# A hybrid decoder step on one core: three edits to what GpSimd issues and to where one stage's value tiles lie

## Chip, cores and metric

The kernel runs on one core of a Trainium2 chip. The metric is the device time of one launch in microseconds (us). Three runs are timed and their median counts; one further execution is profiled, and all rows below are from it.

## The reference, cut to what matters

One layer of a decoder step, in float32, for 512 prompt tokens and for 8 samples of 4 new tokens each; all share the weights.

```
x += 0.5 * SwiGLU_1(RMSNorm(x))
h  = RMSNorm(x); [q|k|v|u] = h @ W_in
x += concat(RMSNorm(DilatedAttn(q,k,v)), RMSNorm(S5_GLU(u))) @ W_out
x += 0.5 * SwiGLU_2(RMSNorm(x))
x += sigmoid(RMSNorm(x) @ W_gate) * (p @ W_ple)
```

Three places matter here. The prompt's attention (8 heads, 512 x 512, in three dilated branches) adds a bias that depends on distance. The samples' attention multiplies softmax weights with gathered rows of a value cache of 2048 positions. The state-space branch ends in a gated unit `z * sigmoid(z @ w_glu + b)`, whose output is normalised by its mean square over 512 channels.

## The kernel before

All 544 tokens stand in the free dimension, channels on the 128 partitions. Every large product goes through `mm_tile` (line 194): a weight tile is split into a high and a low part (`whi` on ScalarE, line 175; `wlo` on VectorE, line 176) and three products are summed. The program has three parts: the first SwiGLU, a mixed part, and the output projection with the second SwiGLU and the rest.

The change is in the mixed part. There each engine runs its instructions in the order in which the code is written, and that order is given by the hand-written table `ORDER`, which calls steps of several generators in turn: `M`/`E` (a matmul tile and what empties it), `SQ` and `B` (the samples' scores), `SA`/`SB` (state space), `aq`/`at`/`ap` (the prompt's attention: scores and softmax, transposes, products with the values), `O0`/`O1` (`sample_out` for samples 0 to 3 and 4 to 7, called the first and the second group here) and others. An instruction that waits holds back everything behind it on its engine. TensorE is PE in the profile, VectorE DVE, ScalarE ACT, GpSimd POOL; PEld is TensorE's weight load.

What the edits touch:

- `load_bt(hp)` (line 1003) fetches the two bias tiles `bt` (256 KB each) of head pair `hp` from DRAM scratch into buffers of the pool `sp5`, 8 buffers that `L`, `pt`, `kb1` and `kt1` share. It is called once before the first unit of `att_q` and then behind the last of the four units of each head pair. Line 1020 reads the tiles; lines 1022 and 1025 are the two passes of the softmax on ScalarE.
- `sample_out(gr)` runs nine steps n = 0 to 8 per group. Each multiplies two value tiles `vv` (e = 0, 1; 512 KB each, line 1178) with weights in `pz` (line 1191). `load(n + 1)` stands ahead of the products of step n. The tiles lie in `wkp`, 6 buffers of which `pz` holds one.
- `sample_scores` streams 32 key tiles `kk` (512 KB, line 1073) through the 4 buffers of `kkp` and query rows `qb` (line 1088) through 2; line 1099 multiplies and line 1100 reduces. All this is done before the second group's first step.
- `glu(m)` (four tiles) squares its output on ScalarE (line 251 for the first, 254 for the others) and adds squares in `Stat.add` (line 255). Line 1220 makes the gated output, line 299 (ScalarE) and line 300 (VectorE) split it.

GpSimd has no other work in the mixed part than to issue the loads of `kk`, `kb1`, `qb`, `bt` and `vv`, in the order of the table, and to add the squares of the gated unit. Weights and results go through SyncE's queue.

Of the kernel before, what the change touches and what calls it, by code (L numbers as in the profile page):

```python
# [18 lines left out]
P = 128  # L19
# [9 lines left out]
DA = 512  # L29
# [73 lines left out]
def decoder_step(ctx: ExitStack, tc: tile.TileContext, a: dict, o: list):  # L103
    nc = tc.nc
    V, A, PE, SP, Q = nc.vector, nc.scalar, nc.tensor, nc.sync, nc.gpsimd

    def dram(t, off, dims):
        return bass.AP(tensor=t.tensor, offset=t.offset + off, ap=dims)
# [6 lines left out]
    def sb(pool, shape, name, dt=F32, **kw):  # L115
        return pool.tile(shape, dt, name=name, **kw)

    qD = dpool.tile([NS, DA], F32, name="qD")
    btD = dpool.tile([NH, P, 641], F32, name="btD")
# [192 lines left out]
    def s2(shape, name, dt=F32):  # L312
        return cur["s2"].tile(shape, dt, name=name, tag="s2")

    def psm(shape=None, name="sm"):
        return cur["sm"].tile(shape or [P, 512], F32, name=name, tag="sm")
# [425 lines left out]
    with ExitStack() as st:  # L742
# [7 lines left out]
        wk = lambda shape, name: wkp.tile(shape, F32, name=name, tag="wk")  # L750
        s5 = lambda shape, name: sp5.tile(shape, F32, name=name, tag="s5")
        kk2 = lambda name: kkp.tile([P, 2, DA], F32, name=name, tag="kk")
# [245 lines left out]
        bts, Ls, pts = {}, {}, {}  # L998

        def load_bt(hp):  # L1000
            for e in range(2):
                bts[hp, e] = s5([P, 512], "bt")
                Q.dma_start(bts[hp, e], dram(btD, (2 * hp + e) * P * 641 + 127, [[640, P], [1, 512]]))

        def att_q():
            load_bt(0)
            yield
            for u, (hp, i) in enumerate(units):
                w = (i + 1) * P
                pss, mns = [], []  # L1010
                for e in range(2):
                    pr = slice(64 * e, 64 * e + 64)
                    ps = psm()
                    PE.matmul(ps[:, :w], qT[pr, hp, i * P:(i + 1) * P], kT[pr, hp, 0:w], start=True, stop=True)
                    pss.append(ps)
                for e in range(2):
                    Ls[u, e] = L = s5([P, 512], "L")
                    mn = sb(small, [P, 4], "mn", bufs=4)
                    mns.append(mn)
                    V.tensor_tensor_reduce(L[:, :w], pss[e][:, :w], bts[hp, e][:, 512 - w:], -1.0, 3e38, ALU.add,  # L1020
                                           ALU.min, mn[:, 0:1])
                    A.activation(L[:, :w], L[:, :w], AF.Exp, scale=-1.0, bias=mn[:, 0:1], accum_out=mn[:, 1:2])  # L1022
                for e in range(2):
                    V.reciprocal(mns[e][:, 2:3], mns[e][:, 1:2])
                    A.activation(Ls[u, e][:, :w], Ls[u, e][:, :w], AF.Copy, scale=mns[e][:, 2:3])
                if i == 3 and hp < 3:
                    load_bt(hp + 1)
                yield
# [104 lines left out]
        def sample_out(gr):  # L1133
            sc = scs[gr]
            s3 = lambda i, n=P: sc[:n, i].rearrange("p b (t h) -> p (b t) h", h=NH)
            bq = lambda t: t[:, None, :].to_broadcast([P, 16, NH])
            fs = lambda i, n=P: sc[:n, i].rearrange("p b x -> p (b x)")
            V.tensor_tensor(s3(0), s3(0), bq(bfar), ALU.add)
            V.tensor_tensor(s3(1), s3(1), bq(bnear), ALU.add)
            mx = s2([P, P], "mx")  # L1140
            V.tensor_tensor(mx, fs(1), fs(2), ALU.max)
            V.tensor_tensor(mx, mx, fs(0), ALU.max)
            V.tensor_tensor(mx[:NS], mx[:NS], fs(3, NS), ALU.max)
            yield
            ps = psm()
            PE.transpose(ps[:, :P], mx, ident)
            m1 = sb(small, [P, 4], "m1", bufs=2)
            V.tensor_reduce(m1[:, 0:1], ps[:, :P], AX.X, ALU.max)
            dg = sb(small, [P, P], "diag", bufs=2)
            V.tensor_scalar(dg, ident, m1[:, 0:1], None, ALU.mult)  # L1150
            yield
            pm = psm()
            PE.matmul(pm[:, :P], ones, dg, start=True, stop=True)
            for i, n_ in ((0, P), (1, P), (2, P), (3, NS)):
                V.tensor_tensor(fs(i, n_), fs(i, n_), pm[:n_, :P], ALU.subtract)
            pz = wk([P, 2, 4, 160], "pz")
            pz = [pz[:, i] for i in range(2)]
            dv = lambda t: t.rearrange("p b (t x) -> p b t x", x=40)[:, :, :, 0:8]
            s4v = lambda i, n=P: sc[:n, i].rearrange("p b (t h) -> p b t h", h=NH)
            for i in range(2):  # L1160
                V.memset(pz[i], 0.0)
                A.activation(dv(pz[i]), s4v(i), AF.Exp)
            A.activation(fs(2), fs(2), AF.Exp)
            A.activation(fs(3, NS), fs(3, NS), AF.Exp)
            yield
            su = s2([P, 4, 4, 8], "su")
            V.tensor_tensor(su, s4v(2), dv(pz[1]), ALU.add)
            V.tensor_tensor(su, su, dv(pz[0]), ALU.add)
            V.tensor_tensor(su[:NS], su[:NS], s4v(3, NS), ALU.add)
            order = [None] + [(j, f) for j in range(DS) for f in range(2)]  # L1170
            vld = {}

            def load(n):
                if n < len(order):
                    r0, step = (1920, 1) if n == 0 else ((order[n][0], 16), (1536 + order[n][0], 4))[order[n][1]]
                    vld[n] = [wk([P, 2, DA], "vv") for _ in range(2)]
                    for e in range(2):
                        Q.dma_start(vld[n][e], dram(cv, ((4 * gr + 2 * e) * PAST + r0) * DA,  # L1178
                                                    [[step * DA, P], [PAST * DA, 2], [1, DA]]))
            load(0)  # L1180
            yield
            ps = psm()
            PE.matmul(ps[:, 0:1], su.rearrange("p b t h -> p (b t h)"), ones[:, 0:1], start=True, stop=True)
            V.reciprocal(m1[:, 1:2], ps[:, 0:1])
            po = psm([P, 512], "po")
            for n, jf in enumerate(order):
                load(n + 1)
                v_ = vld.pop(n)
                for b in range(4):
                    lt = sc[:, 2, b] if n == 0 else pz[jf[1]][:, b, 32 * jf[0]:32 * jf[0] + 32]  # L1190
                    PE.matmul(po[32 * b:32 * b + 32, :], lt, v_[b // 2][:, b % 2, :], start=n == 0, stop=n == len(order) - 1)  # L1191
                if n == 0:
                    for b in range(4):
                        PE.matmul(po[32 * b:32 * b + 32, :], sc[:NS, 3, b], vs, start=False, stop=False)
                yield
            rv = s2([P, NH, HD], "rvv")
            V.scalar_tensor_tensor(rv, po.rearrange("p (h d) -> p h d", d=HD), m1[:, 1:2],
                                   sel_h[:, :, None].to_broadcast([P, NH, HD]), ALU.mult, ALU.mult)
            yield
            pf = psm([P, 4, 16], "pf")  # L1200
            for m in range(4):
                PE.matmul(pf[:, m, :], rv[:, 2 * m:2 * m + 2, :].rearrange("p h d -> p (h d)"), sel_t, start=True, stop=True)
            V.tensor_copy(att[:, :, S + 16 * gr:S + 16 * gr + 16], pf)
            yield

        ssm_st, att_st = Stat(DA, (Q,)), Stat(DA)
        att_st.accs.append(sb(small, [P, NT], "sacc", bufs=2))
        att_sq = att_st.accs[0][:, :S]
        rs = {1: ssm_st, 0: att_st}
# [247 lines left out]
def run_tile(nc, args, outs):  # L1457
    with tile.TileContext(nc, schedule_with_timeline_sim=TS) as tc:
        with tc.manual_schedule(engines=ENG):
            decoder_step(tc, args, outs)  # L1460
# [18 lines left out]
```

## Time and profile before

| | |
|---|---|
| timed runs, us | 1302.9, 1295.39, 1298.36 (median 1298.36) |
| profiled execution, us | 1290.02 |
| its span, us | 1288.2 |
| busy share of the span: TensorE, VectorE, ScalarE, GpSimd | 94%, 55%, 35%, 9% |
| mixed part in the span, about | 440 to 770 us |

The span is the time from the first to the last record of the profile; 1.8 us of the profiled execution lie around it. The busy share is an average: TensorE is at its peak in both SwiGLU parts and below it in the mixed part.

### The profile page before, as it was taken

The page shows a single profiled execution, that of the slowest core. Times are in us where ns is not written, and L with a number is a line of the kernel's source. Part 1 is how long each engine was busy: PE and PEld are TensorE (multiplying, and loading weights), DVE is VectorE, ACT ScalarE, POOL GpSimd, SP SyncE. Part 2 cuts the span into 40 slices and gives each one's busy share as a digit, 9 for nine tenths or more (in the row PEclk, how much of TensorE's full clock was granted, in tenths as well). Part 3 has the DMA queues.
Part 4 walks back from the last instruction along what each step waited for, and adds up shares of the span by engine and source line. Part 5 has one row for each costly group of instructions (what it writes and reads, how often), then busy time and mean ns, then how long its engine had stood idle before and what let it go on. Part 6 is the DMA issues. An engine that isn't in the chain of part 4 may idle for free.

```text
span 1288.2 us, 23223 instructions
## 1 busy us (share of the span) xinstructions
PE 1208.3 (94%) x9518; PEld 1142.4 (89%) x9518; DVE 713.5 (55%) x1499; ACT 446.1 (35%) x889; POOL 121.8 (9%) x195
## 2 busy tenths in 40 slices
PE   8999999999999999994769889999999999999995
PEld 7899999999999988983645449999999999999994
DVE  5544478476447638777775548444433444444455
ACT  5333322322233323121754445333322223333344
POOL 2200000233000112110123311000000000000000
PEclk8999999999999998996979989999999999999998
DMA  8484566668546549766358855445566455222321
GB/s 248 134 260 147 173 217 226 227 198 258 191 167 207 170 138 299 233 203 218 91 207 243 255 172 191 155 144 199 174 217 231 153 192 180 80 83 77 93 64 70
DMA packets 207547, 231.30 MB, mean 180 GB/s; under 512 B 8647, under 2 KB 187735, under 8 KB 206416
## 3 DMA queue, kind: packets, MB, share of 16 engines
q1 hardware_dynamic: 189552, 170.35, 40.8%
q0 software_dynamic: 17856, 59.45, 14.3%
q8 instruction: 75, 1.23, 0.4%
q14 instruction: 32, 0.26, 0.1%
q10 hardware_dynamic: 32, 0.01, 0.0%
HBM read 217.46 MB, written 81.89 MB: 232 GB/s over the span
## 4 chain that ended last, share of the span: by engine, by line
PE 81%; DMA 6%; DVE 5%; issue 4%; ACT 3%; POOL 1%; SPq 0%; ACTq 0%; POOLq 0%; DVEq 0%
PE acc L194 72%; DMA vv<-in_cache_v_dram 2%; DMA raw<-in_w_in_dram 1%; PE acc L206 1%; PE acc L1441 1%; DVE kk L1099 1%; DMA raw<-in_ffn_w_up_dram 1%; DMA pc<-pD 1%; PE sm L915 1%; PE po L1191 1%; DMA mm<-mD 1%; PE sm L910 1%; PE sm L263 1%; POOL vv L1178 1%; ACT L L1022 1%
## 5 line engine op out<-in xcount | busy, mean ns | idle before, releaser
L194 PE MATMUL acc<-xh,whi 128*128 128x272 f32 x1888 | 398.5, 292 | 5.9 <-DVE qT L773 1.3
L194 PE MATMUL acc<-xl,whi 128*128 128x272 f32 x1888 | 393.9, 290 | 0.7 <-DVE xl L304 0.3
L194 PE MATMUL acc<-xh,wlo 128*128 128x272 f32 x1888 | 393.4, 289 | 0.9 <-DVE wlo L176 0.9
L175 ACT CAST whi<-raw 128x512 fp32r<-128x512 f32 (+2 forms) x348 | 208.3, 606 | 531.1 <-PE acc L194 462.0
L176 DVE TENSOR_TENSOR wlo<-raw,whi 128x512 fp32r<-128x512 f32 (+2 forms) x348 | 231.1, 671 | 200.7 <-ACT whi L175 198.2
L194 PEld LDWEIGHTS acc<-xh,whi 128*128 128x128 f32 x1888 | 297.4, 189 | 12.0 <-issue 4.0
L194 PEld LDWEIGHTS acc<-xl,whi 128*128 128x128 f32 x1888 | 299.0, 190 | 1.9 <-DVE xl L304 0.8
L194 PEld LDWEIGHTS acc<-xh,wlo 128*128 128x128 f32 x1888 | 297.7, 189 | 1.4 <-DVE wlo L176 1.3
L194 PE MATMUL acc<-hh,whi 128*128 128x272 f32 x704 | 145.7, 288 | 0.0
L194 PE MATMUL acc<-hh,wlo 128*128 128x272 f32 x704 | 145.3, 288 | 0.0
L194 PE MATMUL acc<-hl,whi 128*128 128x272 f32 x704 | 145.2, 288 | 0.0
L194 PEld LDWEIGHTS acc<-hh,whi 128*128 128x128 f32 x704 | 110.7, 188 | 0.0
L194 PEld LDWEIGHTS acc<-hh,wlo 128*128 128x128 f32 x704 | 110.7, 188 | 0.0
L194 PEld LDWEIGHTS acc<-hl,whi 128*128 128x128 f32 x704 | 110.5, 188 | 0.0
L362 DVE TENSOR_TENSOR s<-acc,rstd 128x544 f32<-128x544 f32 x44 | 31.9, 724 | 87.3 <-PE acc L194 87.3
L356 DVE TENSOR_TENSOR s<-acc,rstd 128x544 f32<-128x544 f32 x44 | 31.9, 724 | 72.1 <-PE acc L194 65.9
L303 ACT CAST hh<-s 128x544 fp32r<-128x544 f32 x44 | 28.5, 647 | 78.9 <-DVE s L363 78.9
L304 DVE TENSOR_TENSOR hl<-s,hh 128x544 fp32r<-128x544 f32 x44 | 31.9, 725 | 27.3 <-ACT hh L303 27.3
L370 DVE SCALAR_TENSOR_TENSOR x<-acc,x 128x544 f32<-128x544 f32 x32 | 23.2, 725 | 36.0 <-PE acc L194 36.0
L1099 DVE TENSOR_TENSOR kk<-kk,qb 128x1024 f32<-128x1024 f32 x32 | 38.9, 1217 | 5.6 <-DMA qb<-qD 5.6
L1100 DVE TENSOR_REDUCE sc<-kk 128x16 f32<-128x1024 f32 x32 | 39.0, 1220 | 1.1
L357 ACT ACTIVATE s<-s 128x544 f32<-128x544 f32 x44 | 29.0, 659 | 11.5 <-DVE s L356 11.2
(397 smaller groups left out, 1116.6 us busy)
## 6 DMA issues: line engine op xcount, KB each, us to landing
out_dram<-in_cache_k_dram SPq DMA_DIRECT2D x32, 1022.0 KB, 7.0
out_dram<-in_cache_v_dram SPq DMA_DIRECT2D x32, 1022.0 KB, 6.0
raw<-in_ffn_w_gate_dram SPq DMA_DIRECT2D x44, 512.0 KB, 4.0
raw<-in_ffn_w_up_dram SPq DMA_DIRECT2D x44, 512.0 KB, 4.0
vv<-in_cache_v_dram POOLq DMA_DIRECT2D x36, 512.0 KB, 6.4
raw<-in_ffn_w_down_dram SPq DMA_DIRECT2D x32, 512.0 KB, 3.8
kk<-in_cache_k_dram POOLq DMA_DIRECT2D x32, 512.0 KB, 5.8
raw<-in_w_in_dram SPq DMA_DIRECT2D x16, 512.0 KB, 8.8
```

The source lines that it names most:

```text
L175: A.copy(hi[:, :len(p), :], r)
L176: V.tensor_tensor(lo[:, :len(p), :], r, hi[:, :len(p), :].bitcast(F32), ALU.subtract)
L194: PE.matmul(ps[:, h, :HT], wt[:, j, :], z[:, h * HT:(h + 1) * HT], start=done == 0 and n == 0, stop=done == len(ks) - 1 and n == 2)
L206: PE.matmul(ps[:, h, :HT], wt[:, j, :], z[:, h * HT:(h + 1) * HT], start=hf == 0 and j == 0 and n == 0, stop=hf == 1 and j == 3 and n == 2)
L303: A.copy(hi, src)
L304: V.tensor_tensor(lo, src, hi.bitcast(F32), ALU.subtract)
L356: V.tensor_tensor(v2(g1), pg[:, :, :HT], v2(rstd()), ALU.mult)
L357: A.activation(g1, g1, AF.Silu)
L362: V.tensor_tensor(v2(u1), pu[:, :, :HT], v2(rstd()), ALU.mult)
L370: V.scalar_tensor_tensor(v2(x[:, m, :]), ps[:, :, :HT], 0.5, v2(x[:, m, :]), ALU.mult, ALU.add)
L1099: V.tensor_tensor(t_, t_, qbs[n // 2], ALU.mult)
L1100: V.tensor_reduce(scs[b // 4][:, f, b % 4, 16 * jp:16 * jp + 16], t_.rearrange("p f (h d) -> p (f h) d", d=HD), AX.X, ALU.add)
```

## The change

Each edit is one expression.

```diff
         def load_bt(hp):
             for e in range(2):
                 bts[hp, e] = s5([P, 512], "bt")
-                Q.dma_start(bts[hp, e], dram(btD, ...))
+                A.dma_start(bts[hp, e], dram(btD, ...))
...
-                    vld[n] = [wk([P, 2, DA], "vv") for _ in range(2)]
+                    vld[n] = [kk2("vv") if gr else wk([P, 2, DA], "vv") for _ in range(2)]
...
-        ssm_st, att_st = Stat(DA, (Q,)), Stat(DA)
+        ssm_st, att_st = Stat(DA), Stat(DA)
```

`Q` is GpSimd, `A` ScalarE, and `Stat` without a second argument adds on VectorE. So the bias tiles are issued by ScalarE's queue, the second group's value tiles lie in the four buffers of the key stream, and three adds of squares move to VectorE.

GpSimd's queue at the end of the mixed part (`bt` bias tiles, `qb` query rows, `kk` keys, `vv` values, with the number of issues that follow each other):

```order
-L1003 DMA bt<-btD 128x512 x2
-L1088 DMA qb<-qD 128x1024
-L1073 DMA kk<-in_cache_k_dram 128x1024
-L1178 DMA vv<-in_cache_v_dram 128x2x512 x2
-L1003 DMA bt<-btD 128x512 x2
-L1178 DMA vv<-in_cache_v_dram 128x2x512 x18
-L1003 DMA bt<-btD 128x512 x2
-L1178 DMA vv<-in_cache_v_dram 128x2x512 x16
+L1178 DMA vv<-in_cache_v_dram 128x2x512 x36
```

The 36 issues of value tiles, 18 for each group, now follow each other with no bias tile between them.

ScalarE where the third head pair's tiles are fetched, behind the softmax of the second head pair's last unit (`L`, `mn`):

```order
 L1022 ACTIVATE L,mn<-L,mn 128x512 x2
 L1025 ACTIVATE L<-L,mn 128x512 x2
+L1003 DMA bt<-btD 128x512 x2
 L1063 COPY qT<-po 128x128
 L175 CAST whi<-raw 128x512
```

Two issues stand between the softmax and the copies and weight casts that follow it; the other three pairs of issues stand in the same way, the first of them behind line 918.

VectorE in the second and third tile of the gated unit (`sacc` is the sum of squares, `s` scratch, `xh` and `xl` the split output):

```order
 L1219 TENSOR_TENSOR s_7035<-xh_88,xl_90 128x544
 L1220 TENSOR_TENSOR s_7033<-s_7033,s_7035 128x544
+L255 TENSOR_TENSOR sacc<-sacc,s_7038 128x544
 L300 SCALAR_TENSOR_TENSOR xl_91<-s_7033,gains,xh_89 128x544
 L176 TENSOR_TENSOR wlo<-raw,whi 128x512
 L1219 TENSOR_TENSOR s_7076<-xh_88,xl_90 128x544
 L1220 TENSOR_TENSOR s_7074<-s_7074,s_7076 128x544
+L255 TENSOR_TENSOR sacc<-sacc,s_7079 128x544
 L300 SCALAR_TENSOR_TENSOR xl_91<-s_7074,gains,xh_89 128x544
```

The add stands between the gated output and its split; the fourth tile has it in the same place.

## Rows read from the trace of the kernel before

**Rows 1.** The page's first part: busy us, share, instructions of each engine.
```profile
PE 1208.3 (94%) x9518; PEld 1142.4 (89%) x9518; DVE 713.5 (55%) x1499; ACT 446.1 (35%) x889; POOL 121.8 (9%) x195
```

**Rows 2.** Windows of 40 us: PE, PEld, DVE, ACT, POOL busy; clock; DMA share; GB/s.
```profile
680.00:720.00 40.00, 36.88 (x271) 22.19 (x271) 23.68 (x55) 17.93 (x46) 12.58 (x19) 1.00 0.82 243
720.00:760.00 40.00, 32.63 (x230) 16.91 (x230) 17.48 (x54) 19.55 (x52) 13.79 (x20) 0.96 0.80 248
```

**Rows 3.** The chain that ended last, 655 to 698 us: start, length, what.
```profile
655.63 1.41 DVE xl L300
...
665.11 19.23 issue
...
689.09 8.89 DMA vv<-in_cache_v_dram
```

**Rows 4.** Timeline of POOL: start, length, instruction, count, [idle before it <-releaser].
```profile
663.65 1.46 POOL L1178 DMA_DIRECT2D vv<-in_cache_v_dram  x2
684.35 1.16 POOL L1003 DMA_DIRECT2D bt<-btD  x2 [19.25 <-DVE mn L1020]
...
689.09 1.42 POOL L1178 DMA_DIRECT2D vv<-in_cache_v_dram  x2 [1.45 <-PE po L1191]
...
731.79 1.42 POOL L1178 DMA_DIRECT2D vv<-in_cache_v_dram  x2 [4.57 <-PE po L1191]
...
746.41 2.83 POOL L1178 DMA_DIRECT2D vv<-in_cache_v_dram  x4 [6.05 <-PE po L1191]
```

**Rows 5.** All waits, 440 to 840 us, the row of L1191: total us, times, longest.
```profile
PEld po L1191 <- DMA vv<-in_cache_v_dram: 11.6, 8, 3.6
```

**Rows 6.** Timeline of PEld at the sample products: six of those eight waits.
```profile
692.67 0.14 PEld L1191 LDWEIGHTS po<-vv,pz 128*32 128x32 f32 x4 [0.53 <-DMA vv<-in_cache_v_dram]
...
695.08 0.14 PEld L1191 LDWEIGHTS po<-vv,pz 128*32 128x32 f32 x4 [0.79 <-DMA vv<-in_cache_v_dram]
698.02 0.14 PEld L1191 LDWEIGHTS po<-vv,pz 128*32 128x32 f32 x4 [2.79 <-DMA vv<-in_cache_v_dram]
...
706.38 0.14 PEld L1191 LDWEIGHTS po<-vv,pz 128*32 128x32 f32 x4 [0.99 <-DMA vv<-in_cache_v_dram]
...
721.90 0.14 PEld L1191 LDWEIGHTS po<-vv,pz 128*32 128x32 f32 x4 [1.96 <-DMA vv<-in_cache_v_dram]
...
738.28 0.14 PEld L1191 LDWEIGHTS po<-vv,pz 128*32 128x32 f32 x4 [3.56 <-DMA vv<-in_cache_v_dram]
```

**Rows 7.** Timeline of PE: the second group's step 0 and step 5.
```profile
730.43 1.06 PE L1191 MATMUL po<-vv,sc 128*32 128x512 f32 x8
...
751.71 1.93 PE L1191 MATMUL po<-vv,pz 128*32 128x512 f32 x8
```

**Rows 8.** Loads of vv from issue to landing: all 36; the pair from 719.91.
```profile
DMA to landing us min/median/max: 4.1/6.4/9.9
DMA to landing us min/median/max: 5.2/5.5/5.8
```

**Rows 9.** Timelines of DVE, POOL and ACT in the gated unit.
```profile
630.38 0.78 DVE L300 SCALAR_TENSOR_TENSOR xl<-s,gains,xh 128x544 fp32r<-128x544 f32 x1 [1.37 <-ACT xh L299]
...
634.67 1.35 DVE L300 SCALAR_TENSOR_TENSOR xl<-s,gains,xh 128x544 fp32r<-128x544 f32 x1 [1.37 <-ACT xh L299]
...
634.08 1.35 POOL L255 TENSOR_TENSOR sacc<-sacc,s 128x544 f32<-128x544 f32 x1 [13.84 <-ACT s L254]
...
633.34 0.66 ACT L254 ACTIVATE s<-s 128x544 f32<-128x544 f32 x1 [1.32 <-DVE s L1220]
```

**Rows 10.** Timelines of ACT's queue, ACT and DVE at bias tiles and softmax.
```profile
0.74 0.43 ACTq L685 DMA_DIRECT2D gt<-in_norm_ffn_dram  x1
...
732.61 1.32 ACT L1025 ACTIVATE L<-L,mn 128x512 f32<-128x512 f32 x2
...
739.79 0.29 DVE L1020 CUSTOM_DVE_ANT_0 L<-sm,bt 128x128 f32<-128x128 f32 x1 [5.42 <-PE sm L1014]
```

**Rows 11.** Loads of bt from issue to landing: the pair from 684.35.
```profile
DMA to landing us min/median/max: 3.2/3.2/3.2
```

More of the change, by code (lines that the diff above doesn't have):

```diff
@@ L1002, in load_bt @@
                 bts[hp, e] = s5([P, 512], "bt")
-                Q.dma_start(bts[hp, e], dram(btD, (2 * hp + e) * P * 641 + 127, [[640, P], [1, 512]]))
+                A.dma_start(bts[hp, e], dram(btD, (2 * hp + e) * P * 641 + 127, [[640, P], [1, 512]]))
         def att_q():
```

## The prediction

> **What bounds the kernel now.** I read the page's first part, then windows of 40 us, the chain that ended last, the timelines of GpSimd and TensorE's weight loads in the windows where TensorE is not full, and last the gated unit. TensorE is busy for 94% of the span and GpSimd for 9% [rows 1], so an edit on GpSimd is worth something only where TensorE waits for what GpSimd issues. That place is in rows 2: between 680 and 760 us TensorE is idle for 3.1 and 7.4 us, at nearly full clock (1.00 and 0.96), and its weight loads, which follow each other more densely at its peak, are down to 22 and 17 of 40 us. The chain runs there through GpSimd: 19.23 us in which it issues nothing, then a load of value tiles of 8.89 us [rows 3]. Its timeline says why. The first two value tiles go out at 663.65, then two bias tiles are next in the queue and wait until 684.35, when VectorE has read the old tiles; everything behind stands still for 19.25 us although buffers for three more value tiles are free, since these follow at once at 685.51 (684.35 + 1.16) [rows 4]. TensorE then waits for value tiles eight times, 11.6 us in all [rows 5]. In the first group these are 0.53 (step 1), 0.79 and 2.79 (the halves of step 2), 0.99 (step 4) and 1.96 (step 8); in the second 3.56 (step 2) [rows 6], and the remaining 11.6 - 10.6 = 1.0 near its end.
>
> **The gated unit.** Three of GpSimd's adds move to VectorE. The split of line 300 lasts 0.78 us when GpSimd is quiet, 1.35 when the add runs beside it (634.08 to 635.43), and 1.41 in the fourth tile [rows 9, 3]. Without the add I give it 0.78. The add itself, a VectorE operation of the same 128 x 544, I price at 0.78 too; its input is ready when line 254 ends (633.34 + 0.66 = 634.00), and VectorE idles there for 1.37 us until 634.67 [rows 9]. So it ends near 634.8 and pushes the split by 0.1: per tile -0.57 + 0.1, or about -0.5. Line 300 stands on the chain [rows 3], so three tiles give **-1.5**. Bounds: +0.3 if the split stays slow for another reason, -1.9 if nothing is pushed (3 x 0.63).
>
> **The first group.** With the bias tiles gone from the queue, nothing holds the value tiles of step 1 and the first of step 2: they go out behind the first two at about 665 and land by 675 even at the slowest 9.9 us [rows 4, 8], long before step 1 at 692. The sixth tile, the second half of step 2, has no free buffer (six, less `pz`) until step 0 has read its first; it is issued at 689.09 in either version [rows 4]. Before, it lands 8.89 us later [rows 3], behind the three tiles just issued; now these are out of its way, and a pair that is not crowded needs 5.2 to 5.8 us [rows 8]: 694.3 to 694.9. Without the waits ahead of it TensorE would want it at 698.02 - 2.79 - 0.79 - 0.53 = 693.9 [rows 6]. So of the 4.1 us, 0.4 to 1.0 stay: -3.4. The 0.99 of step 4 is the same backlog one round later and goes with it. The 1.96 of step 8 stays: its last tile waits for step 6's buffer in both versions. Together **-4.4**. Bounds: 0 if the sixth tile still needs 8.9 us (then it is as late as before, and the earlier waits were hidden in it), -5.1 if it needs 4.1 [rows 8].
>
> Here I weigh a rule against the rows. The 36 loads of 512 KB take 4.1 to 9.9 us from issue to landing, 6.4 in the median [rows 8]. The Trainium skill (DMA: Bandwidth & Descriptors, "Anatomy of one DMA") gives 2.0 us plus the bytes over 436 GB/s for a transfer that GpSimd issues, an estimate of 3.2 us here; no row is that short. By it the late halves would come 2 us earlier than I count, and the sum would be near -9 in place of -4.4. I go by the rows.
>
> **The second group.** Its tiles move from five usable buffers to four. The first four are free once the key stream has ended, so steps 0 and 1 are loaded ahead in any case. Step 2 now waits for step 0 with both halves: the second goes out 0.71 us (half of 1.42) behind 731.79, at 732.5, and lands after 5.2 to 5.8 us at 737.7 to 738.3, where before it came at 738.28 [rows 4, 6, 8]. No change. Later each load goes out one place further back. At 746.41 four loads leave in a row when step 3 frees buffers [rows 4]; step 5's second half will be the second of them, not the first, so 747.1 + 5.8 = 752.9, wanted half a step into step 5 at 751.71 + 0.5 [rows 7]: a new wait of 0.6. I count about as much again at steps 6 and 8, where the remaining 1.0 us of waiting already sits: **+1.5**. Bounds: -1.7 if landings fall to 4.1 (step 2 then at 736.6), +12 by the third rival.
>
> **ScalarE's queue.** An issue there took 0.43 us [rows 10], so four pairs cost 0.86 each. ScalarE works for 18 to 20 of 40 us here [rows 2], and behind the softmax come copies and weight casts that TensorE wants several microseconds later: **0**. Uncovered it would be 3 x 0.86 = 2.6, since the first pair stands before any softmax. The tiles are now fetched just in time: the last pair can leave at 732.61 + 1.32 = 733.9 and is out at 734.8; with 3.2 us to land [rows 11] it is there at 738.0, and its first reader starts at 739.79 [rows 10]. That leaves 1.8 us, and less if step 2 of the second group comes earlier. The value tiles never wait for it now.
>
> **Sum.** -1.5 - 4.4 + 1.5 + 0 = -4.4. The profiled execution took 1290.02 us (span 1288.2 and 1.8 around it), so 1285.6 in its place; it lies 8.3 us under the median of the runs shown, 1298.36, and on that median the forecast is **1294.0**.
>
> **The rivals.**
> *Short landings.* With less crowding all late loads could land in 4.1 us: -1.5 in the gated unit, -5.1, and -1.7 at step 2 of the second group, in all -8.3 or 1290.1. For it: the 4.1 us row exists. Against: the DMA engines are busy for 0.80 to 0.82 of both windows [rows 2], with weights and output in the same stream.
> *The transfers are the limit, not the queue.* At a DMA share of 0.82 [rows 2] the same bytes take the same time whoever issues them; then the sixth tile and its successors stay as late as they are, only the gated unit gains, -1.5 or 1296.9. Against: for 19.25 us GpSimd issued nothing with buffers free [rows 4]. The Trainium skill (Trainium Kernel Development and Optimization, "Key Constraints") speaks for this one: the queues of all issuers share 16 DMA engines, and spreading issues over them saves issue time alone.
> *Four buffers are too few* (slower). With four, the loads of a step can only leave when the step two before has read. If a load needs 8.9 us as in rows 3, step 2's second half comes at 741.4, 3.1 us later than before, and steps 4, 6 and 8 can each repeat that: 3.1 to 12.4, in the middle 7.8. The first group then gains nothing, so -1.5 + 1.5 + 7.8 = +7.8, or 1306.2. It decides from landings of about 7 us in the second group, against 5.2 to 5.8 in its quiet pair and 6.4 in the median [rows 8].
>
> **How the numbers follow.** About 0.5%, or 6.5 us, is what a measurement of this kernel can tell from no change. My forecast (a gain of 2 to 6.5 us) has a chance of 0.45, short landings 0.30, the transfer limit 0.15, too few buffers 0.10. Faster by over 0.5% takes the short landings and the edge of the forecast: 0.33; slower 0.07, most of the third rival; the rest, 0.60, within 0.5%. The range goes from the first rival less 3 us of scatter (the lowest run lies 3.0 under the median) to the second plus 4.5 (the highest run): 1287 to 1302; that leaves out the third rival and the extremes.
>
> **What would show it.** After the change line 300 should last under 0.9 us in all four tiles, with line 255 on VectorE ahead of it. Value tiles two to five should be issued before 670 us; the wait of 2.79 at the first group's step 2 should be under 1.0 and the 0.99 gone, while about 2 us stay at its step 8 and 3 to 4 at the second group's step 2. TensorE's idle time between 680 and 720 should fall by some 3 us. The sum is wrong if the sixth tile still takes over 7 us to land, if VectorE's line 1020 waits for `bt`, or if the second group's waits add up to more than 7 us.

## The result and the profile after

The change makes the kernel slower: 1312.41 us in the median of four runs (1310.24 to 1318.6) against 1296.88 (1295.26 to 1302.9) for the kernel before on the same chip. The ratio is 1.0119 with a 95% interval of 1.0086 to 1.0153, so about 15.4 us. The forecast was 1294.0, in a range of 1287 to 1302.

The profiled execution of after is its slowest, 1318.6 us, and that of before its fastest, so the two spans differ by 27.3 us. Of these, 9.3 are there at 540 us, ahead of the first transfer that the change touches (the first bias pair, issued at 544.87 us before), and still 9.3 at 552; I leave them out and compare stretches behind that.

The page's first part and two windows of 5 us of after, then two windows of before (PE, PEld, DVE, ACT, POOL busy; clock; DMA share; GB/s), each at the place where TensorE waits for `mm`:

```profile
PE 1219.2 (93%) x9518; PEld 1149.4 (87%) x9518; DVE 713.4 (54%) x1502; ACT 446.7 (34%) x889; POOL 112.1 (9%) x184
...
575.00:580.00 5.00, 0.00 (x0) 0.00 (x0) 0.00 (x0) 0.00 (x0) 0.00 (x0) 0.55 1.05 377
580.00:585.00 5.00, 4.49 (x25) 3.25 (x26) 2.43 (x3) 1.14 (x2) 0.00 (x0) 0.50 0.11 27
```

```profile
560.00:565.00 5.00, 3.96 (x33) 3.70 (x31) 2.32 (x2) 0.00 (x0) 1.59 (x3) 1.00 1.04 374
565.00:570.00 5.00, 4.04 (x26) 2.93 (x27) 0.00 (x0) 0.00 (x0) 0.00 (x0) 0.66 0.96 343
```

TensorE is busy for 10.9 us more [rows 1] with the same instructions, so some of them run slower. For five microseconds no engine works at all while the DMA engines are full, and behind that TensorE runs at the lower of its two clock levels (granted clock 0.50). What it waits for is on the chain that ended last, in order of time:

```profile
566.89 13.49 DMA mm<-mD
580.51 1.10 PE sm L910 x4
...
588.04 9.14 DMA raw<-in_w_glu_dram
...
715.61 8.44 DMA vv<-in_cache_v_dram
...
752.64 9.00 DMA vv<-in_cache_v_dram
```

`mm` is SyncE's load for the state space; it took 8.15 us before and takes 13.49 now. Before, on its chain and on TensorE's timeline:

```profile
557.67 8.15 DMA mm<-mD
...
565.96 0.66 PE L910 MATMUL sm<-mm,UC 128*72 128x128 f32 x4 [2.00 <-DMA mm<-mD]
```

The timelines of ACT's queue and of DVE, and the waits of 440 to 860 us (total, times, longest), name the cause that is nearest:

```profile
566.21 0.86 ACTq L1003 DMA_DIRECT2D bt<-btD  x2
...
680.31 1.49 ACTq L1003 DMA_DIRECT2D bt<-btD  x1
```

```profile
652.01 0.73 DVE L255 TENSOR_TENSOR sacc<-sacc,s 128x544 f32<-128x544 f32 x1 [0.73 <-ACT s L254]
652.65 0.78 DVE L300 SCALAR_TENSOR_TENSOR xl<-s,gains,xh 128x544 fp32r<-128x544 f32 x1
...
688.43 0.29 DVE L1020 CUSTOM_DVE_ANT_0 L<-sm,bt 128x128 f32<-128x128 f32 x1 [3.06 <-DMA bt<-btD]
690.40 0.29 DVE L1020 CUSTOM_DVE_ANT_0 L<-sm,bt 128x128 f32<-128x128 f32 x1 [1.67 <-DMA bt<-btD]
```

```profile
PEld po L1191 <- DMA vv<-in_cache_v_dram: 18.4, 13, 3.9
...
PE sm L910 <- DMA mm<-mD: 9.7, 3, 7.3
DVE L L1020 <- DMA bt<-btD: 4.7, 2, 3.1
```

Before, GpSimd issued the first bias pair at 544.87, in a quieter time (DMA share 0.45 from 545 to 555 us). ScalarE comes to it only behind line 918, at 566.21, 0.6 us after SyncE begins to issue `om`, `mm` and `raw`. The waits for value tiles grow from 11.6 to 18.4 us [rows 5]: in the first group they are 7.0 us in all where they were 7.1, in the second 11.5 where they were 4.6. GpSimd's timeline and the weight loads of the second group's step 2 show where:

```profile
677.43 3.56 POOL L1178 DMA_DIRECT2D vv<-in_cache_v_dram  x5 [0.17 <-issue]
...
734.66 3.55 POOL L1178 DMA_DIRECT2D vv<-in_cache_v_dram  x5 [3.59 <-PE po L1191]
751.94 1.41 POOL L1178 DMA_DIRECT2D vv<-in_cache_v_dram  x2 [13.73 <-PE po L1191]
```

```profile
757.62 0.14 PEld L1191 LDWEIGHTS po<-vv,pz 128*32 128x32 f32 x4 [3.07 <-DMA vv<-in_cache_v_dram]
...
761.68 0.19 PEld L1191 LDWEIGHTS po<-vv,pz 128*32 128x32 f32 x4 [3.91 <-DMA vv<-in_cache_v_dram]
```

The first group's tiles leave five at once and early, as forecast [rows 4]. In the second group step 2 waits for both halves, 3.07 and 3.91 us, where it waited 3.56 for one [rows 6].

### The profile page after: what moved, and what is told of

The parts are those of the page before. It is cut to its first block, busy times and chain, and to the rows that moved or that the text cites. A ratio compares the mean times of both kernels' runs of the same rounds, so it can differ in the third digit from the quotient of the medians.

```text
span 1315.5 us, 23221 instructions
## 1 busy us (share of the span) xinstructions
PE 1219.2 (93%) x9518; PEld 1149.4 (87%) x9518; DVE 713.4 (54%) x1502; ACT 446.7 (34%) x889; POOL 112.1 (9%) x184
## 4 chain that ended last, share of the span: by engine, by line
PE 80%; DMA 8%; issue 6%; DVE 3%; ACT 2%; POOL 1%; SPq 0%; ACTq 0%; POOLq 0%; DVEq 0%
PE acc L194 72%; DMA vv<-in_cache_v_dram 3%; DMA raw<-in_w_in_dram 1%; DMA mm<-mD 1%; PE acc L206 1%; DMA raw<-in_ffn_w_up_dram 1%; PE acc L1441 1%; DMA raw<-in_w_glu_dram 1%; PE sm L910 1%; DMA pc<-pD 1%; PE sm L915 1%; DVE kk L1099 1%; PE sm L263 1%; POOL vv L1178 0%; PE po L1191 0%
## 5 line engine op out<-in xcount | busy, mean ns | idle before, releaser
L1191 PE MATMUL po<-vv,pz 128*32 128x512 f32 x128 | 27.2, 646 | 9.8 <-DMA vv<-in_cache_v_dram 9.8
```

## The experiments

Times are medians, ratios against before on the same chip with their 95% interval; where I give microseconds, it is the ratio less 1 times 1298; the intervals are 2 to 4 us wide either way. Unless said otherwise each kernel is before with the edit shown. **Theory:** the loss is the first bias pair, moved to a bad moment, and the four buffers of the second group. **Rivals:** the four buffers alone; ScalarE's issues themselves; differences between runs.

**only_bt**, all bias pairs on ScalarE:
```
-                Q.dma_start(bts[hp, e], ...
+                A.dma_start(bts[hp, e], ...
```


> Only line 1003 is changed: all four pairs of bias tiles are issued by ScalarE; adds and value buffers as before. Theory (the first pair, issued by ScalarE some 20 us later and in the middle of the raw and mm loads, costs about 8 us around 560 to 620 us; the second pair is late for line 1020 and costs 3; the first group's value tiles give 3 back): 1296.9 + 8, about 1305, with TensorE waiting over 5 us for mm at line 910. Rival 1 (the four buffers of the second group are the whole loss): 4 us faster than before, about 1293, line 910 as before. Rival 2 (the two profiles only differ by the run): within 2 us of before.

1308.37, ratio 1.0066 [1.0040, 1.0092]: +8.6 us. Its `mm` comes late as in after, and the matmuls behind it last 1.10 us for four where they lasted 0.66:
```profile
582.26 1.10 PE L910 MATMUL sm<-mm,UC 128*72 128x128 f32 x4 [7.70 <-DMA mm<-mD]
```

**bt_late**, the first pair left with GpSimd: `(A if hp else Q).dma_start(bts[hp, e], ...`

> As only_bt, but the first pair of bias tiles (hp = 0) stays with GpSimd; pairs 2 to 4 go to ScalarE. Theory: the 8 us around 560 to 620 us are gone, what is left is the late second pair (+3) against the first group's gain (-3): within 2 us of before, about 1297, and 8 us below only_bt. Rival 1: the same as only_bt, about 1293. Rival 2: within 2 us of before and of only_bt.

1301.25, ratio 1.0010 [0.9992, 1.0028]. The 7.3 us between these two are the first pair's. The other three pairs come out even: the first group gains, but the second and the fourth pair are late, the fourth by 6.35 us:
```profile
747.63 0.29 DVE L1020 CUSTOM_DVE_ANT_0 L<-sm,bt 128x128 f32<-128x128 f32 x1 [6.35 <-DMA bt<-btD]
```

**only_kk**, the second group's tiles in four key buffers:
```
-                    vld[n] = [wk([P, 2, DA], "vv") for _ in range(2)]
+                    vld[n] = [kk2("vv") if gr else wk([P, 2, DA], "vv") for _ in range(2)]
```


> Only line 1176 is changed: the second group's value tiles come from the key stream's four buffers; bias tiles and adds as before. Theory: steps 2 and 4 to 8 of the second group wait longer, +6 us, about 1303, first group as before. Rival 1: +15 us, about 1312. The prediction's own step: +1.5, about 1298.4.

1306.87, ratio 1.0065 [1.0039, 1.0091]: +8.4 us. Step 2 of the second group, and the 5 us behind its first half:
```profile
744.85 1.92 PE L1191 MATMUL po<-vv,pz 128*32 128x512 f32 x4 [3.05 <-DMA vv<-in_cache_v_dram]
748.07 1.92 PE L1191 MATMUL po<-vv,pz 128*32 128x512 f32 x4 [1.30 <-DMA vv<-in_cache_v_dram]
...
745.00:750.00 5.00, 3.70 (x10) 0.31 (x8) 0.00 (x0) 0.00 (x0) 0.70 (x1) 0.50 0.86 266
```
Both halves are late, TensorE falls to the lower clock, and its four matmuls last 1.92 us in place of 1.05.

**only_adds**, the gated unit's adds on VectorE: `Stat(DA, (Q,))` becomes `Stat(DA)`.

> Only line 1206 is changed: the gated unit's three adds move from GpSimd to VectorE. Theory: the add stands right ahead of line 300 on VectorE and pushes it by about as much as line 300 itself gets shorter, so -0.4 us in the gated unit, within 1 us of before, about 1296.5. The prediction's own step: -1.5 us, 1295.4. Rival 3 (VectorE with more work is late elsewhere): over 2 us slower.

1294.99, ratio 0.9968 [0.9945, 0.9992]: more than I expected; its profile shows 1.1 us in the gated unit.

**first_early**, only_bt with the first pair issued sooner:
```
+        for n, t in enumerate(ORDER.split()):
+            if n == 62:
+                load_bt(0)
```


> As only_bt (all four bias pairs on ScalarE), but ScalarE issues the first pair ahead of the table load of line 918, some 8 us sooner, where the DMA engines stood at a share of 0.01. Theory (it is the moment that costs): the wait for mm at line 910 is back under 3.5 us, the 10 us between 552 and 580 us are gone, 1 to 2 us above before as bt_late was. Rival (ScalarE's DMA queue beside SyncE's and GpSimd's costs, whenever it is used): as only_bt, some 8.6 us above before.

1299.75, ratio 1.0009 [0.9988, 1.0029]. The same pair from the same engine, at 555.20, 8.1 us ahead of `om` (563.29), costs nothing that shows; line 910 is back:
```profile
572.38 0.63 PE L910 MATMUL sm<-mm,UC 128*72 128x128 f32 x4 [1.42 <-DMA mm<-mD]
```

**first_pool_late**, all pairs on GpSimd, the first at `n == 67`:

> All four bias pairs stay with GpSimd, but the first is issued some 13 us later, behind a load of line 1088 and one of line 1073, just as SyncE issues om and mm. Theory (the moment): TensorE waits 4 to 8 us for mm at line 910 and the kernel is 5 to 9 us slower than before, with no issue on ScalarE at all. Rival (ScalarE's queue): within 2 us of before.

1303.07, ratio 1.0033 [1.0011, 1.0056]: +4.3, less than expected.
```profile
577.84 1.10 PE L910 MATMUL sm<-mm,UC 128*72 128x128 f32 x4 [4.52 <-DMA mm<-mD]
```
So the moment is a part of it. That the engine's queue is another is not shown by this: GpSimd issues the pair 0.1 us behind `mm` (567.10 and 567.01), where only_bt's ScalarE issues it 0.7 us ahead (567.53 and 568.20), so the order differs too.

**first_sync**, the first pair on SyncE, which issues it behind `mm`: `(Q if hp else SP).dma_start(bts[hp, e], ...`

> From before, the first bias pair is issued by SyncE, behind mm and ahead of raw in its own queue, at the moment at which only_bt's ScalarE issues it; pairs 2 to 4 and the rest as before. Theory (at that moment it is in the way of what SyncE loads, and a queue of its own puts it ahead of mm): mm is no longer overtaken, the wait at line 910 is under 3.5 us; raw comes later by the pair's bytes, 1 to 3 us. In all 1 to 3 us slower than before. Rival (half a megabyte more in the DMA engines costs the 8 us in whatever order): 6 us or more slower, wait for mm 5 us or more.

1304.69, ratio 1.0037 [1.0016, 1.0058]: +4.8, more than theory and less than the rival. `mm` is no longer late, `raw` is (ScalarE waits 15.17 us for it, 13.02 before):
```profile
569.43 0.63 PE L910 MATMUL sm<-mm,UC 128*72 128x128 f32 x4 [1.29 <-DMA mm<-mD]
...
577.30 1.14 ACT L175 CAST whi<-raw 128x512 fp32r<-128x512 f32 x2 [15.17 <-DMA raw<-in_w_in_dram]
```

**kk_wk**, nine buffers: `[kk2("vv") if gr and e else wk([P, 2, DA], "vv") for e in range(2)]`

> Only line 1176 is changed: of each step's two tiles of the second group one comes from the key stream's buffers and one from the old ones, nine in all. Theory (four buffers are too few, the buffers themselves are as good): the second group waits under 3 us for its tiles, 2 us faster than before, and some 10 us faster than only_kk. Rival (key buffers come free late, or loads into them are slow): 4 us or more slower than before.

1298.01, ratio 1.0004 [0.9979, 1.0028]. The loss of only_kk is gone, so it was their number; but no gain, since step 2 still waits 2.80 us with buffers free:
```profile
742.81 0.14 PEld L1191 LDWEIGHTS po<-vv,pz 128*32 128x32 f32 x4 [2.80 <-DMA vv<-in_cache_v_dram]
```

**bias_in_kk**, pairs 2 to 4 in a key buffer each, issued one unit sooner:
```
+            big_bt = kk2("bt") if hp else None
+                bts[hp, e] = big_bt[:, e, :] if hp else s5([P, 512], "bt")
-                if i == 3 and hp < 3:
+                if i == 2 and hp < 3:
```


> Bias pairs 2 to 4 get a key-stream buffer each (both tiles in one) and are issued by GpSimd one unit sooner (at i == 2); adds and value buffers as before. They need not wait for the readers of the old pair, so GpSimd's 19 us without an issue are gone. Theory (that queue held the first group's tiles): the gain of 3.3 us that bt_late shows in the first group, without its late second pair: 3 us faster than before. Rival (the transfers are the limit): within 1 us of before.

1307.45, ratio 1.0071 [1.0045, 1.0096]. My premise failed: the third pair still waits 16.52 us in GpSimd's queue, and since it now stands ahead of all value tiles, five of them wait behind it:
```profile
692.80 1.08 POOL L1004 DMA_DIRECT2D bt<-btD  x2 [16.52 <-DVE mn L1021]
693.92 3.55 POOL L1179 DMA_DIRECT2D vv<-in_cache_v_dram  x5
```

**third_late** and **third_adds**: pair 3 issued by GpSimd at the head of its first unit; the second has the adds on VectorE too.
```
-                if i == 3 and hp < 3:
+                if i == 3 and hp in (0, 2):
+                if i == 0 and hp == 2:
+                    load_bt(hp)
```


> From before, one thing moved: the third bias pair (hp = 2) is issued by GpSimd at the head of its first unit, behind the first group's first four value tiles in the queue, not ahead of two of them. Everything else as before. Theory (in GpSimd's queue the first group's tiles stood behind that pair): the wait at the first group's step 2 falls and 2 to 3 us are gained, about 1297. Rival (the DMA engines are the limit there): within 1 us of before. A third way (the pair itself now comes late for its readers): line 1020 waits for bt and it is slower.

> third_late and the gated unit's three adds on VectorE as well. If only_adds' 4.2 us are its own, 4 us below third_late, about 1293; if they were scatter (its profile showed 1 us), about 1 us below it.

1304.85, ratio 1.0037 [1.0012, 1.0062], and 1304.95, 1.0033 [1.0008, 1.0057]: the third way, or nearly. The pair got another buffer and waits 24.80 us; value tiles behind it are later still:
```profile
696.74 1.09 POOL L1003 DMA_DIRECT2D bt<-btD  x2 [24.80 <-PE sm L1050]
...
705.02 0.19 PEld L1193 LDWEIGHTS po<-vv,pz 128*32 128x32 f32 x4 [5.63 <-DMA vv<-in_cache_v_dram]
```

**mended**, the changed kernel with first_early's and kk_wk's edits:

> The changed kernel with two things mended: the first bias pair leaves ahead of line 918's table load as in first_early, and the second group takes one tile of each step from the key stream's buffers and one from the old ones as in kk_wk. Theory (the loss is the sum of the first pair's moment and the four buffers): adds -4, first_early +0.1, kk_wk -1.6: 1294 to 1298, some 15 us below the changed kernel. Rival (ScalarE's issues cost by themselves): still 5 us or more above before.

1302.69, ratio 1.0037 [1.0012, 1.0062]: +4.8, and my expectation failed. The number is nearly the rival's, but the trace shows a late transfer, not the issues: the waits for value tiles are short (6.0 us in all), but the fourth bias pair, which ScalarE issues at 740.55 behind nine of them (727.32 to 733.67, the slowest 14.0 us from issue to landing), is late for line 1019 (before's 1020), and TensorE for what follows:
```profile
748.14 0.29 DVE L1019 CUSTOM_DVE_ANT_0 L<-sm,bt 128x128 f32<-128x128 f32 x1 [6.16 <-DMA bt<-btD]
...
752.56 0.14 PEld L1037 LDWEIGHTS sm<-ident,L 128*128 128x128 f32 x1 [4.86 <-ACT L L1024]
```

**adds_bt** and **adds_kk**, the changed kernel without the edit of line 1176, and without that of line 1003:

> The changed kernel without its edit of line 1176: bias pairs on ScalarE and the adds on VectorE, value tiles in the old buffers. If the parts add up: 8.6 - 4.2, about 4 us above before, 1304, and so 11 us below the changed kernel, which is then what four buffers cost in company. If four buffers cost less beside the moved bias pairs (since loads leave sooner): 8 us or more above before.

> The changed kernel without its edit of line 1003: four key buffers for the second group and the adds on VectorE, all bias pairs with GpSimd. If the parts add up: 7.7 - 1.5, about 6 us slower than before, 1304, which leaves 9 us of the changed kernel's 15.5 to the bias pairs. If the four buffers are worse without the moved pairs: 10 us or more slower.

1306.66, ratio 1.0051 [1.0028, 1.0075], and 1306.32, 1.0056 [1.0031, 1.0081]. The parts add up within their intervals: 8.6 + 8.4 - 4.2 = 12.8 for 15.4; taken from the changed kernel, line 1176 is worth 8.8 (15.4 - 6.6) and line 1003 8.1 (15.4 - 7.3). The 15.4 rests on four runs against four, so these two are good to about 5 us.

**third_act** and **third_act_adds**, the third pair alone on ScalarE, without and with the adds on VectorE: `(A if hp == 2 else Q).dma_start(bts[hp, e], ...`

> From before, the third bias pair alone (hp = 2) is issued by ScalarE; pairs 1, 2 and 4 stay with GpSimd. Theory (this is the pair that holds GpSimd's queue for 19 us in front of the first group's tiles, and on ScalarE it landed in 3 us with nothing waiting for it): the first group's 3.3 us gain that only_bt, bt_late and first_early show, without their late second and fourth pairs: 3 us faster than before. Rival (the three transfers that then leave early crowd out something else): within 1 us of before or slower.

> third_act and the gated unit's three adds on VectorE. Theory: 3.3 + 1.5, about 4.8 us faster than before, 1293 to 1295. Rival: the adds as only_adds' median had them (4.2) and no gain from the pair, which gives nearly the same time; then third_act of this call is not faster than before, and the profile shows the wait at the first group's step 2 as it was.

1295.55, ratio 0.9972 [0.9946, 0.9999], and 1296.72, 0.9963 [0.9935, 0.9991]: both faster than before, by 3.6 and 4.8, the first only just clear of no change. The five tiles leave early, and no reader waits for the pair. The waits at step 1 and at the first half of step 2 are gone; of the 2.79 us at its second half 1.85 stay:
```profile
667.53 3.56 POOL L1178 DMA_DIRECT2D vv<-in_cache_v_dram  x5
...
699.68 0.14 PEld L1191 LDWEIGHTS po<-vv,pz 128*32 128x32 f32 x4 [1.85 <-DMA vv<-in_cache_v_dram]
```

**third_act_both**, third_act_adds with kk_wk's nine buffers:

> third_act_adds with the second group's tiles taken from nine buffers as in kk_wk (one of each step from the key stream's, one from the old ones); pairs 1, 2 and 4 of the bias stay with GpSimd, so the fourth is not overtaken as in the mended kernel. Theory (with nine buffers the second group's waits fall from about 5 us to under 3 once nothing else is late): 2 us below third_act_adds, 5 to 6 us faster than before, 1294 to 1295. Rival (the second group is held by the transfers, as kk_wk's wait of 2.80 us says): the same as third_act_adds, 3.5 us faster than before.

1292.34 against 1298.57, ratio 0.9957 [0.9931, 0.9982]: 5.6 us faster than before and the lowest ratio of all; the intervals of third_act_adds and only_adds overlap with it. The waits of 440 to 840 us, against [rows 5]:
```profile
PEld po L1191 <- DMA vv<-in_cache_v_dram: 7.2, 4, 2.8
```

## Why the prediction was wrong

The theory of the experiments holds. only_bt loses 8.6 us with the old buffers, so the four buffers alone are not the loss; first_early issues all four pairs on ScalarE and loses nothing that shows, so the issues themselves are not; and the loss is too large and too steady for a difference between runs. Two steps of the prediction failed: ScalarE's queue was priced by its issues, and step 2 of the second group was called "No change".

To see where each kernel gains, take one TensorE instruction, its start in a profile less its start in that of before; the table has how much this grows, in us, between places named by before's clock (so 9.6 is 18.9 at 580 less 9.3 at 552). Stretches far from what a kernel moves show up to 2.5 either way in one profile, first_sync 4.0 (see "Still open"). Between 500 and 540 us, ahead of every edit, the profiles of all kernels here fall 0 to 7.3 us behind that of before.

| kernel | 552-580 | 580-630 | 630-660 | 660-704 | 704-725 | 725-780 |
|---|---|---|---|---|---|---|
| changed | +9.6 | -0.2 | -1.1 | -0.2 | +2.7 | +6.4 |
| only_bt | +10.4 | -1.0 | 0.0 | -0.4 | +1.5 | +2.0 |
| bt_late | -0.4 | -0.4 | 0.0 | -0.2 | +1.1 | +2.0 |
| only_kk | +2.1 | +0.6 | -0.5 | +0.7 | +3.5 | +4.4 |
| adds_kk | -0.3 | -0.7 | -1.3 | +0.4 | +0.8 | +9.9 |
| third_act | +2.5 | -2.0 | 0.0 | -2.2 | -0.2 | +1.2 |
| third_act_adds | -0.5 | 0.0 | -1.1 | -2.8 | +0.1 | +1.3 |

**ScalarE's queue, priced at 0: wrong, and half of the loss.** The text counted the 0.43 us of an issue and dismissed the first pair, since it "stands before any softmax". It never asked where in time each pair would fall, and what transfers it would meet there. The first pair fell among SyncE's loads and costs 7.3 us (only_bt less bt_late), or 9.6 to 10.4 in the profiles: 5.3 of them are `mm`'s longer landing (13.49 less 8.15); of the rest in the changed kernel about 3.5 are the later `raw` (of `w_glu`) and 0.8 the lower clock behind the idle time. An issue there took 0.33 to 1.49 us, but that is not what it cost. "Just in time" was named as a risk for the last pair alone; the second was late too. Two of the sum's three signs of being wrong came true: "VectorE's line 1020 waits for `bt`" (4.7 us), and the second group's waits add up to 11.5 us, over its 7.

**The second group, +1.5: the mechanism right, the size wrong by 7.** Four buffers cost 8.4 us (only_kk), or 8.8 beside the other edits. The failed step is "No change" at step 2: from step 1 to its second half TensorE's start moves by 2.6, 3.2 and 3.3 us in only_kk, adds_kk and the changed kernel, and in no other profile does it come more than 0.2 later. The step took 5.2 to 5.8 us from the quiet pair issued at 719.91 [rows 8], but the two tiles issued at 731.79 and 732.50 were there to be read in the trace of before (the first also in [rows 4, 6], as 738.28 - 731.79):
```profile
DMA to landing us min/median/max: 6.4/6.8/7.2
```
With 7.2 the second half comes at 739.7, 1.4 us later than before. In after those two took 5.64 and 9.00 us (751.94 to 757.58, 752.64 to 761.64), which is what the third rival had priced at this step: 8.9 and 3.1 later. That rival, with a chance of 0.10 and outside the range, was the case; its repeats at steps 4, 6 and 8 came as waits of 0.5 to 1.9 us.

Nor did the sum reckon with the clock. In only_kk and adds_kk it had fallen by the end of the first of the two waits, in after by the end of the second (granted clock 0.53 from 762 to 767 us), and what follows runs at half speed for some microseconds: from step 1 to 745 us the start moves by 4.2, 5.9 and 5.5 us in these three. That is not a matter of two waits: behind one wait of about the same length at this step the clock stayed up in before (3.56 us) and fell in third_act (3.42 us), which has the old buffers:
```profile
739.00:744.00 5.00, 5.00 (x48) 4.42 (x46) 2.43 (x9) 3.42 (x10) 0.71 (x1) 1.00 0.97 355
```
```profile
740.00:745.00 5.00, 5.00 (x35) 3.45 (x31) 1.21 (x7) 2.73 (x9) 0.70 (x1) 0.66 0.99 357
```
One more cost the sum put at nothing: in the four key buffers the second group's first tiles need not wait, and leave at once behind the first group's last tile (five in a row at 734.66). That tile lands after 5.9, 6.0 and 7.3 us in only_kk, adds_kk and after, where it took 4.9, and step 8 of the first group starts about 1 us later. That kk_wk loses nothing shows that the number of buffers is the cause.

**The first group, -4.4: the mechanism right, the size too large.** The tiles left early and TensorE's start moved by -3.0 to -3.3 us around step 2 in the changed kernel, only_bt and bt_late, close to the -3.4 counted there; step 2's wait became 0.98 where it was 2.79. But the 0.99 of step 4 did not go (1.34), new waits came at steps 6 and 7 (1.22 and 0.68), and step 8 waits 2.56 for 1.96. Over the whole group the start moves by only -0.3 us in the changed kernel, and by -1.6 to -2.7 in the eight others whose third pair is on ScalarE. And the late second pair (line 1020, 3.06 and 1.67 us) cost 2.6 just ahead, so the changed kernel has -0.2 from 660 to 704; third_act, which moves only the pair that blocked the queue, keeps 2.2 of it. So the queue was the limit at step 2, and the rival that the transfers were is refuted for this place. The Trainium skill (Trainium Kernel Development and Optimization, "Key Constraints") would have the choice of queue save issue time alone; here 19.25 us of standing still in an in-order queue counted for more, and the measurement decides.

**The gated unit, -1.5: right.** Line 300 lasts 0.78 us in all four tiles of after, where it took up to 1.41 [rows 3, 9], and the stretch is shorter by 1.1 to 1.7 us in each of the eight profiled kernels with the adds on VectorE. In the medians the pairs with and without them differ by -4.2, -1.9, -1.2, -0.5 and -1.2 us, each with an interval of 3 or more either way. (The sum's 0.6 at the second group's step 5 was misread: half of the 1.93 us in [rows 7] is 0.97, not 0.5, which leaves 0.2. Nothing hangs on it.)

**Still open.** Half a megabyte at the 377 GB/s of those windows is 1.4 us, not the 5.3 that `mm` came later. The runs speak for the queue as a part of it: issued 0.6 us behind `mm` in SyncE's own queue the pair leaves TensorE a wait of 1.29 us, issued 0.1 us behind it in GpSimd's one of 4.52. Issued ahead of `mm` in ScalarE's it is 7.70; whether the place ahead or the queue makes this last step was not tried. The Trainium skill (DMA: Bandwidth & Descriptors, "Queues, rings and completion order") says that each DMA engine takes turns between the queues that have work, packet by packet; a further queue with work would then shorten SyncE's turns. That fits the order of the three numbers, but how the 5.3 us come about no run here measures. Why first_sync's profile loses a further 4.0 us and first_pool_late's 2.0 from 660 to 704, far from what they move, was not tried.

## What to carry to other kernels

Moving a transfer to another engine's queue moves it in time: look up where that engine's program comes to it and what is in flight then, and price it by the loads of that moment, not by its issue. Take the price of a landing from the very transfers that the change delays, in the trace before; the row from a quieter place beside it said "No change" here for a step that came 3 us later and, with the clock behind it, 4 to 6. If one transfer blocks an in-order queue, move that one alone.

## What the hardware showed that was not expected

- Before, the three bias pairs that stand waiting in GpSimd's queue land 3.0 to 3.3 us after their issue, with the value tiles behind them held back too; the fourth pair from ScalarE took 7.6 us in bt_late, behind value tiles that had left ahead of it. So the blocking had kept its way clear.
- After 5 us in which TensorE did nothing, its granted clock was 0.50, the lower level: four matmuls of line 910 took 1.10 us for 0.66. Behind a wait of 3.05 us in only_kk four of line 1191 took 1.92 for 1.05. A wait can cost more than its own length, and whether it does differed between two profiles with about the same wait (3.56 and 3.42 us, above).
